# Nearest-neighbour upsampling on one core: the rows of x owned in two blocks instead of one

## The chip, the core and the metric

The kernel runs on one core of one Trainium2 chip. The metric is the device time of one execution in microseconds (us). The kernel before takes 197.16 us, the median of three runs that lie between 197.04 and 197.44 us. Lower is better.

## What is computed

The input x has the shape (16, 64, 64, 64) and the type float32. Each element of x becomes a square of two by two equal elements of the output, which has the shape (16, 64, 128, 128):

```python
for i in range(new_h):
    for j in range(new_w):
        result[:, :, i, j] = x[:, :, i // 2, j // 2].copy()
```

No arithmetic is done. 16.78 MB are read from DRAM and 67.11 MB are written to it.

## The kernel before

x is looked at as 65,536 rows of 64 floats (256 bytes each). One row of x makes 1,024 bytes of output: the widened row, twice. Partition p of the 128 partitions of SBUF owns 512 rows that follow each other, the rows 512p to 512p + 511. In x the first rows of two neighbouring partitions are therefore 128 KB apart, and in the output 512 KB.

One SBUF tile, `mem`, holds 207 KB a partition: a free region of 79 expanded rows at its start, and behind it the 512 rows of x (`xt`).

**Loads** (L149 to L151). SyncE (SP in the profile) issues three DMAs: rows 0 to 8 of each partition (256 KB in all, here called the head), rows 8 to 256 (7936 KB, the middle load) and rows 256 to 512 (8192 KB, the third load). `begin_before_barrier` (L13 to L33) takes the first `EARLY = 3` instructions of SP in the kernel's body and puts them ahead of the program's opening barrier.

**Expansion and stores** (L160 to L172). The rows are worked off in nine groups of 62, 32, 48, 64, 50, 64, 64, 64 and 64 rows a partition. For each group VectorE (DVE) copies the rows of x, broadcast in two axes, into an expanded buffer `u` inside `mem` (L170), and SP issues one DMA that stores `u` (L171). The buffers alternate between the start of `mem` and the place where rows of x have been used up (L162), so that the copy of a group waits for stores of earlier groups. The first group is copied in two parts, rows 0 to 31 and 31 to 62; its store waits for both. All twelve DMAs are issued by SP and go through one queue.

**The end** (L36 to L107). `close_early` rearranges the closing instructions: all semaphores but that of the last store are waited for and cleared early, and SP waits alone for the last store.

Of the kernel before, what the change touches and what calls it, by code (L numbers as in the profile page):

```python
# [1 line left out]

# [4 lines left out]

EARLY = 3  # L10


def begin_before_barrier(nc):  # L13

    blocks = nc.main_func.blocks
    main, body = blocks[0], blocks[1]
    sp = mybir.EngineType.SP
    loads = [i for i in body.instructions if i.engine == sp][:EARLY]  # L20
    for load in loads:
        assert isinstance(load, mybir.InstDMACopy), type(load)
        assert not (load.sync_info and load.sync_info.on_wait)
    names = [i.name for i in loads]
    body.instructions = [i for i in body.instructions if i.name not in names]
    kept = list(main.instructions)
    at = next(
        n
        for n, i in enumerate(kept)
        if i.engine == sp and isinstance(i, mybir.InstDrain)  # L30
    )
    kept[at:at] = loads
    main.instructions = kept  # L33


def close_early(nc):  # L36

    blocks = nc.main_func.blocks  # L40
    sp, pool = mybir.EngineType.SP, mybir.EngineType.Pool
    stores = [
        i
        for i in blocks[1].instructions
        if i.engine == sp and isinstance(i, mybir.InstDMACopy)
    ]
    last = stores[-1].sync_info.on_update[0].id

    end = list(blocks[-1].instructions)
    wait = end[0]  # L50
    assert wait.engine == sp and isinstance(wait, mybir.InstDrain)
    waits = list(wait.sync_info.on_wait)
    assert len({w.id for w in waits}) == len(waits) > 2
    assert all(w.wait_mode == "sem-ge-imm" for w in waits)

    mine = [i for i in end if i.engine == pool]
    kinds = [type(i).__name__ for i in mine]
    assert kinds == [
        "InstDrain",
        "InstEventSemaphore",  # L60
        "InstEventSemaphore",
        "InstDrain",
        "InstISA",
        "InstDrain",
        "InstEventSemaphore",
        "InstEventSemaphore",
    ], kinds
    d0, gather0, release0, d1, clear, d2, gather1, release1 = mine


    lo, hi = clear.ant_dict["range_first"], clear.ant_dict["range_last"]
    assert lo <= last <= hi and all(lo <= w.id <= hi for w in waits)
    clears = []
    for a, b in ((lo, last), (last + 1, hi + 1)):
        if a < b:
            clears.append(nc.gpsimd.sem_clear(range(a, b)).ins)

    landed = mybir.InstDrain(
        name=wait.name,
        engine=pool,  # L80
        debug=wait.debug,
        sync_info=mybir.SyncInfo(
            on_wait=[w for w in waits if w.id != last], on_update=[]
        ),
    )
    (w,) = [w for w in waits if w.id == last]
    final = mybir.InstEventSemaphore(
        name=clear.name,
        engine=sp,
        debug=wait.debug,  # L90
        sync_info=mybir.SyncInfo(
            on_wait=[w],
            on_update=[
                mybir.SyncUpdate(
                    sync_type=w.sync_type,
                    id=w.id,
                    ant_name=w.ant_name,
                    update_mode="sem-sub-imm",
                    update_value=w.wait_value,
                )  # L100
            ],
        ),
    )
    others = [i for i in end if i.engine != pool and i is not wait]
    blocks[-1].instructions = others + [
        d0, gather0, release0, gather1, release1, d1, landed, *clears, d2, final
    ]  # L107


@with_exitstack  # L110
def kernel(
    ctx: ExitStack,
    tc: tile.TileContext,
    x: bass.AP,
    scale_factor: int,
    out: bass.AP,
):
    nc = tc.nc
    nc.at_finalize(begin_before_barrier)
    nc.at_finalize(close_early)  # L120
    P = nc.NUM_PARTITIONS
    s = int(scale_factor)
    B, C, H, W = x.shape
    R = B * C * H // P
    fdt = x.dtype

    xp = x.rearrange("b c h w -> (b c h) w").rearrange("(p r) w -> p r w", p=P)
    op = out.rearrange("b c (h hd) w -> (b c h) (hd w)", hd=s).rearrange(  # L130
        "(p r) w -> p r w", p=P
    )

    rows = [62, 32, 48, 64, 50, 64, 64, 64, 64]
    GROW = s * s
    FREE = 79
    WF = FREE * GROW * W  # L140
    assert sum(rows) == R
    mem_pool = ctx.enter_context(tc.tile_pool(name="mem", bufs=1))
    mem = mem_pool.tile([P, WF + R * W], fdt, name="mem")
    xt = mem[:, WF:].rearrange("p (r w) -> p r w", r=R)

    HEAD = 8
    cuts = [0, HEAD, R // 2, R]  # L149
    for lo, hi in zip(cuts, cuts[1:]):  # L150
        nc.sync.dma_start(out=xt[:, lo:hi], in_=xp[:, lo:hi])  # L151

    def expanded(r0, r1):
        return (
            xt[:, r0:r1].unsqueeze(2).unsqueeze(4).to_broadcast([P, r1 - r0, s, W, s])
        )

    r0 = 0
    before = (0, 0)
    for n, k in enumerate(rows):  # L160
        size = k * GROW * W
        at = 0 if n % 2 == 0 else WF + r0 * W - size  # L162
        assert at >= before[1] or at + size <= before[0]
        before = (at, at + size)
        u = mem[:, at : at + size].rearrange(
            "p (k a w b) -> p k a w b", k=k, a=s, w=W
        )
        parts = [0, 31, k] if n == 0 else [0, k]
        for a, b in zip(parts, parts[1:]):
            nc.vector.tensor_copy(out=u[:, a:b], in_=expanded(r0 + a, r0 + b))  # L170
        nc.sync.dma_start(out=op[:, r0 : r0 + k, :], in_=u)  # L171
        r0 += k  # L172


# [1 line left out]
_INS = ['x', 'scale_factor']  # L176
_OUTS = [((16, 64, 128, 128), 'float32')]

_NUMBERS = {'scale_factor': 2}


# [26 lines left out]
```

## Time and profile before

| | |
|---|---|
| median of three runs | 197.16 us (197.04 to 197.44) |
| span of the profiled execution | 195.8 us |
| median time less that span | 1.36 us |
| VectorE busy | 78.0 us, 40% of the span |
| DMA queue: packets, bytes, share of 16 engines' span | 1728, 83.89 MB, 99.2% |
| packets under 512 B, under 2 KB, under 8 KB | 192, 192, 320 |

The span runs from the first to the last instruction of the one profiled execution. The page gives no time of its own for that execution, so the median stands beside its span, and the difference is what lies around the span. A DMA is cut into packets that 16 DMA engines carry; the packets under 512 B are the completion marks, 16 for each of the 12 DMAs, and the 128 between 2 KB and 8 KB are those of the head load (one for each partition, 2,048 B). In a table by stretches of time the columns are: the stretch and its length, busy time and count of each compute engine, the clock, the DMA share (the time of the packets that start in the stretch, over the stretch and 16 engines; it can pass 1) and GB/s (the bytes of the packets that start in it).

### The profile page before, as it was taken

How to read it: one execution, taken by the hardware profiler on the slowest of the kernel's cores; microseconds unless marked ns; L12 is line 12 of the kernel's file. 1: busy time of each engine (PE TensorE's matmuls, PEld its weight loads, DVE VectorE, ACT ScalarE, POOL GpSimd, SP SyncE). 2: the span in 40 equal slices, each digit the busy share in tenths (PEclk: the TensorE clock that was granted, in tenths of full speed). 3: DMA queues.
4: the chain of work that ended last, by engine and by line, in shares of the span. 5: the costliest groups of instructions: out<-in, count | busy, mean ns of one | idle time of the engine just before them, and what ended most of it. 6: DMA issues, size and time to landing. Idle time of an engine off the chain costs nothing.

```text
span 195.8 us, 76 instructions
## 1 busy us (share of the span) xinstructions
DVE 78.0 (40%) x10; POOL 0.2 (0%) x4
## 2 busy tenths in 40 slices
DVE  0000599980007579085008907900890088000000
POOL 0000000000000000000000000000000000000000
DMA  9999999999999999899987989999999999999994
GB/s 456 415 428 415 428 428 428 428 415 415 415 415 428 428 482 482 375 469 495 469 384 345 502 348 455 442 469 482 469 442 428 428 428 442 428 428 428 428 428 214
DMA packets 1728, 83.89 MB, mean 428 GB/s; under 512 B 192, under 2 KB 192, under 8 KB 320
## 3 DMA queue, kind: packets, MB, share of 16 engines
q1 hardware_dynamic: 1728, 83.89, 99.2%
HBM read 16.78 MB, written 67.11 MB: 428 GB/s over the span
## 4 chain that ended last, share of the span: by engine, by line
DMA 60%; DVE 24%; SPq 0%; issue 0%; DVEq 0%
DMA out_dram<-mem 49%; DVE mem L170 24%; DMA mem<-in_x_dram 11%; SPq L151 0%; DVEq L170 0%
## 5 line engine op out<-in xcount | busy, mean ns | idle before, releaser
L170 DVE COPY mem<-mem 128x16384 f32<-128x16384 f32 (+4 forms) x10 | 78.0, 7812 | 87.8 <-DMA out_dram<-mem 65.8
L189 POOL MEMSET const-uint8-127<- 128x1 uint8 x1 | 0.1, 102 | 0.0
L189 POOL MEMSET const-bfloat16-1.0<- 128x1 bf16 x1 | 0.1, 101 | 0.0
L189 POOL MEMSET const-float32-0.0<- 128x1 f32 x1 | 0.1, 98 | 0.2 <-issue 0.2
L189 POOL MEMSET const-float32-1.0<- 128x1 f32 x1 | 0.1, 98 | 0.0
## 6 DMA issues: line engine op xcount, KB each, us to landing
mem<-in_x_dram SPq DMA_DIRECT2D x1, 7936.0 KB, 21.5
out_dram<-mem SPq DMA_DIRECT2D x1, 7936.0 KB, 21.2
out_dram<-mem SPq DMA_DIRECT2D x1, 6400.0 KB, 27.6
out_dram<-mem SPq DMA_DIRECT2D x1, 6144.0 KB, 17.5
out_dram<-mem SPq DMA_DIRECT2D x1, 4096.0 KB, 26.4
mem<-in_x_dram SPq DMA_DIRECT2D x1, 256.0 KB, 2.7
out_dram<-mem SPq DMA_DIRECT2D x5, 29.8
mem<-in_x_dram SPq DMA_DIRECT2D x1, 40.4
```

Of the source, the lines that this page charges most:

```text
L170: nc.vector.tensor_copy(out=u[:, a:b], in_=expanded(r0 + a, r0 + b))
L189: nc = _bacc.Bacc("TRN2", target_bir_lowering=False, num_devices=1)
```

## The change

The ownership of rows is cut in two blocks. Partition p now owns 8 rows in the first 1,024 rows of x (rows 8p to 8p + 7) and 504 rows in the rest (1024 + 504p and on). The head load then reads one stretch of 256 KB of DRAM; in the second block the partitions lie 126 KB apart in x and 504 KB apart in the output. In SBUF nothing moves: the row numbers 0 to 511 of a partition, the groups and the copies are the same. The loads are still three DMAs of the same sizes. The first group has rows of both blocks, so its store becomes two DMAs: rows 8 to 62 first (6912 KB), then rows 0 to 8 (1024 KB, one stretch of the output). There are thirteen DMAs instead of twelve.

```diff
-    xp = x.rearrange("b c h w -> (b c h) w").rearrange("(p r) w -> p r w", p=P)
-    op = out.rearrange("b c (h hd) w -> (b c h) (hd w)", hd=s).rearrange(
-        "(p r) w -> p r w", p=P
-    )
+    xr = x.rearrange("b c h w -> (b c h) w")
+    outr = out.rearrange("b c (h hd) w -> (b c h) (hd w)", hd=s)
+    BLOCKS = [8, 504]
+    assert sum(BLOCKS) == R
+    xb, ob, r0 = [], [], 0
+    for k in BLOCKS:
+        xb.append(xr[P * r0 : P * (r0 + k)].rearrange("(p r) w -> p r w", p=P))
+        ob.append(outr[P * r0 : P * (r0 + k)].rearrange("(p r) w -> p r w", p=P))
+        r0 += k
+
+    def within(views, lo, hi):
+        found, r0 = [], 0
+        for k, v in zip(BLOCKS, views):
+            a, b = max(lo, r0), min(hi, r0 + k)
+            if a < b:
+                found.append((a, b, v[:, a - r0 : b - r0]))
+            r0 += k
+        return found
...
-    HEAD = 8
-    cuts = [0, HEAD, R // 2, R]
-    for lo, hi in zip(cuts, cuts[1:]):
-        nc.sync.dma_start(out=xt[:, lo:hi], in_=xp[:, lo:hi])
+    LOADS = [0, 8, R // 2, R]
+    for lo, hi in zip(LOADS, LOADS[1:]):
+        for a, b, part in within(xb, lo, hi):
+            nc.sync.dma_start(out=xt[:, a:b], in_=part)
...
-        nc.sync.dma_start(out=op[:, r0 : r0 + k, :], in_=u)
+        for a, b, part in reversed(within(ob, r0, r0 + k)):
+            nc.sync.dma_start(out=part, in_=u[:, a - r0 : b - r0])
```

## The prediction

> **What bounds the kernel now.** I read the DMA queue's line of the page first, then the chain of work that ended last, then the DMA issues with their sizes, and last the table by stretches of time around the start and the end.
>
> ```profile
> q1 hardware_dynamic: 1728, 83.89, 99.2%
> ```
>
> The packets fill 99.2% of the 16 engines' span: no compute engine matters unless it lets the queue run dry. The chain gives landings, as a start and a length:
>
> ```profile
> 0.00 0.38 SPq L151
> 0.38 0.05 issue
> 0.43 21.46 DMA mem<-in_x_dram
> ...
> 38.77 21.19 DMA out_dram<-mem
> 59.95 0.02 issue
> 59.98 6.57 DVE mem L170
> 66.55 0.02 issue
> 66.56 17.53 DMA out_dram<-mem
> ...
> 90.97 27.55 DMA out_dram<-mem
> ...
> 127.27 29.89 DMA out_dram<-mem
> ```
>
> ```profile
> mem<-in_x_dram SPq DMA_DIRECT2D x1, 7936.0 KB, 21.5
> out_dram<-mem SPq DMA_DIRECT2D x1, 7936.0 KB, 21.2
> out_dram<-mem SPq DMA_DIRECT2D x1, 6400.0 KB, 27.6
> out_dram<-mem SPq DMA_DIRECT2D x1, 6144.0 KB, 17.5
> out_dram<-mem SPq DMA_DIRECT2D x1, 4096.0 KB, 26.4
> mem<-in_x_dram SPq DMA_DIRECT2D x1, 256.0 KB, 2.7
> ```
>
> The middle load lands at 0.43 + 21.46 = 21.89 us, the first store at 59.96, the third (6144 KB) at 84.09, the fifth (6400 KB) at 118.52, the seventh at 157.16; the span ends at 195.8. Between those marks lie:
>
> - 21.89 to 59.96: the third load (8192 KB) and the first store, 16.52 MB in 38.07 us, 433.8 GB/s
> - 59.96 to 84.09: 10.49 MB in 24.13 us, 434.6 GB/s
> - 84.09 to 118.52: 14.94 MB in 34.43 us, 434.0 GB/s
> - 118.52 to 157.16 and 157.16 to 195.8: 16.78 MB in 38.64 us each, 434.2 GB/s
>
> One pace from 21.89 us to the end, through loads and stores and over every join of two DMAs. Nothing is to be had there. Up to 21.89 us the head and the middle load moved 8.39 MB, which at 434.2 GB/s take 19.32 us; **2.57 us are start-up**, paid once. The table by stretches shows what they are:
>
> ```profile
> 0.00:0.98 0.98, 0.00 (x0) 0.20 (x4) 1.00 0.00 0
> 0.98:1.22 0.24, 0.00 (x0) 0.00 (x0) 1.00 1.31 137
> 1.80:1.91 0.11, 0.00 (x0) 0.00 (x0) 1.00 1.00 391
> 2.41:2.60 0.19, 0.00 (x0) 0.00 (x0) 1.00 0.86 334
> 4.40:4.66 0.26, 0.00 (x0) 0.00 (x0) 1.00 4.54 1953
> 4.66:4.80 0.14, 0.00 (x0) 0.00 (x0) 1.00 7.32 3174
> 4.80:5.13 0.33, 0.00 (x0) 0.00 (x0) 1.00 0.00 0
> 5.13:5.15 0.02, 0.00 (x0) 0.00 (x0) 1.00 7.32 3174
> 57.10:57.24 0.14, 0.00 (x0) 0.00 (x0) 1.00 1.05 453
> 192.30:192.70 0.40, 0.00 (x0) 0.00 (x0) 1.00 5.67 2458
> 192.70:193.00 0.30, 0.00 (x0) 0.00 (x0) 1.00 0.00 0
> 193.00:193.05 0.05, 0.00 (x0) 0.00 (x0) 1.00 3.02 1311
> ```
>
> GB/s times the stretch is bytes, hence packets; share times 16 times the stretch is their time together. No packet starts in the first 0.98 us. In 0.98:1.22 start 32.9 KB, 16 head packets of 2,048 B, taking 1.31 x 16 x 0.24 = 5.03 us, **314 ns each**. In 1.80:1.91 start 21, in 1.76 us: **84 ns each**. So the head's first packets take almost four times what its last ones do. In 2.41:2.60 starts one packet of the middle load (63,488 B) and takes 2.61 us; the one in 57.10:57.24, of the same size but of a store, takes 2.35.
>
> Then count the middle load's second packets, one an engine: eight start in 4.40:4.66, seven in 4.66:4.80, none until 5.13, and the sixteenth in 5.13:5.15. **One engine is a third of a microsecond behind the other fifteen.** At the end it still is: fifteen of the last 65,536 B packets start in 192.30:192.70, none in 192.70:193.00, one in 193.00:193.05. Its packet takes 3.02 x 16 x 0.05 = 2.42 us, and about 0.35 us after that the span is over. All engines carry the same bytes at the same pace, so the engine that leaves the start-up last sets the end.
>
> **The change, part by part.** *The head load.* Same 256 KB, same 128 packets (SBUF takes 2,048 B a partition as before), same issue ahead of the others; only the DRAM addresses draw together. No row shows a load from one stretch. From below: the late engine and the slow first packets have nothing to do with the addresses, gain 0. From above: every engine leaves the start-up as early as the first ones do, 5.14 - 4.40 = 0.74 us. It can also lose, if 16 engines in one stretch get in each other's way; nothing excludes that, and the bound is the rival's below. I take the middle of the pack, because the fifteen other engines went through the same start-up in the same execution and are the nearest row: eight engines are through by 4.66, so the last one comes 5.14 - 4.66 = **0.48 us earlier**. My reason for a gain at all is the 314 against 84 ns: the excess sits where an engine touches DRAM first, at 16 places far apart, and with one stretch these first reads lie close together. This is argued and not shown.
>
> *The middle and third loads and eight of the stores* keep their sizes; their DRAM pitch goes from 128 to 126 KB and from 512 to 504 KB. The load at the one pitch and the stores at the other run at 433.8 and 434.2 GB/s: I count 0. The Trainium skill, page "DMA: Bandwidth & Descriptors", section "Latency and other measured facts", lists copies with a row pitch of 512 KiB at 207 GB/s and with a padded pitch at 214. By that rule the stores' 154.6 us at 434.2 GB/s would shrink by 3.3%, about 5 us by estimate; the trace disagrees so far, since 512 KB pitches already move at 434.2 GB/s beside 433.8 for a stretch that is half load at 128 KB.
>
> *The second store DMA.* Rows 0 to 8 leave as 128 packets of 8,192 B, eight an engine, behind those of rows 8 to 62. The bytes are the same, so what is added is the overhead of eight packets and one completion mark an engine. A 2,048 B packet takes 84 ns, while 2,048 B at a sixteenth of 434.2 GB/s (27.1) take 75.5: at most 8.5 ns a packet, 0.07 us for eight, and from below 0. A mark is a packet too; I give it one more such overhead. I take **0.06 us**, near the upper end.
>
> *The issue of that DMA.* SP is not counted as busy for it; the one issue in the chain took 0.38 us (0.00 on). It follows the first store's issue at 38.77, so SP is free by about 39.6. Behind it waits the second store's issue, which needs VectorE's third copy:
>
> ```profile
> 38.77 4.43 DVE L170 COPY mem<-mem 128x8192 f32<-128x8192 f32 x1
> 43.23 0.34 SPq L171 DMA_DIRECT2D out_dram<-mem  x1
> ```
>
> That is 43.2, so 3.6 us of cover; and the queue has the first 54 rows by then. Cost 0, and if the cover were gone, 0.38.
>
> *The added wait.* The third group's copy (59.98) overwrites the first store's buffer and must now wait for two DMAs. Both land by the time one did, plus the 0.06 above. Behind it stands the third store's issue at 66.56. Its 6144 KB need 14.5 us at the pace and land at 84.09, so it comes to move at about 69.6: 3 us after its issue, of which the 0.98 us before a first packet (the first stretch) must be taken off. Two microseconds hide the 0.06. With no such cover each 0.1 us of delay would be 0.1 us of dry queue.
>
> *The sum.* 195.8 - 0.48 + 0.06 = 195.4 us of span. Around the span lie 197.16 - 195.8 = 1.36 us if the profiled execution was one of the median, so **196.74 us**, 0.21% under it. What is late next is the slowest of the other engines.
>
> **The rivals.**
>
> *The start-up stays (no change).* The late engine's delay may come from how DMAs are handed to the engines and not from DRAM. For it: fifteen engines passed the same head within 0.4 us of each other, and the packet in 2.41:2.60 starts after all head traffic of the table's earlier rows, as if it had waited for its order. Against: the first packets are slow on many engines. Then only the added store counts: 197.16 + 0.06 = 197.22. A partial gain, the late engine catching up with half of its 0.34, gives 197.05. Within 0.2% (196.77 to 197.55, about what a measurement of this kernel can tell from no change) lies all of this.
>
> *Crowding (slower).* Sixteen engines read one 256 KB stretch instead of 16 places, and each packet then takes what only the first take now. Eight packets of 314 ns are 2.5 us an engine, where now the head lies between 0.98 and about 2.4, 1.4 us: 1.1 us more, 198.3. It decides as soon as the head costs 0.4 us more than now, a landing later than 2.7 + 0.4 = 3.1 us after its issue. For it: this addressing occurs nowhere in the trace. Against: 16 engines at equal offsets never disturb each other after 5 us.
>
> *Each DMA has its fixed price (slower).* The head's 256 KB land in 2.7 us, where 0.6 would do at the pace: 2.1 us. If the second store paid that, 197.16 + 2.1 = 199.3. The stretches speak against it: each has a join of two DMAs, none below 433.8 GB/s, where 2.1 us in 24.13 would be 9%. The Trainium skill, page "SBUF — State Buffer", section "The DMA setup-cost knee", has every transfer pay about 2 us and its summary says one DMA and not several; the head's row agrees, the queued stores' rows don't.
>
> *The pitch pays.* Stores 3% faster by some conflict that the trace doesn't show: 154.6 us less 3% is about 4.6 us, 192.5.
>
> *It doesn't do what it says.* The stretch might be carried in fewer, larger packets; the packet count shows it. The time would be that of the forecast or of no change.
>
> **How the numbers follow.** Forecast (start-up shorter by 0.4 to 0.8 us): 0.48. Start-up unchanged or little changed: 0.34. Crowding or any other longer start-up beyond 0.4 us: 0.15. Fixed price: 0.02. Pitch: 0.01. So faster 0.49, same 0.34, slower 0.17. The low end is the upper bound of the gain, 197.16 - 0.74 + 0.06 = 196.48, rounded down to 196.4 for the spread of the runs (0.12 below the median). The high end takes in no change and a start-up worse by some 0.4 us: 197.6. Outside are most of crowding, fixed price and pitch, some 0.17.
>
> **What would show it.** Right: packets 1872 (128 + 16 more), 208 of them under 512 B; the head landing earlier than 2.7 us; the middle load at about 21.4; the sixteen second packets close together and no gap like 4.80:5.13; later stretches still at 434 GB/s. Wrong: an engine still alone behind the others; a head landing past 3 us; a stretch with the two first stores below 433; an idle queue before 66.

## The result, and the profile after

The kernel after takes 197.55 us, the median of 22 runs (197.32 to 197.92), against 197.12 us for the kernel before in 22 runs beside them (196.97 to 197.78). The ratio is 1.002 with a 95% interval of 1.0014 to 1.0026: **0.4 us slower**, where 0.4 us faster was forecast. The profiled execution of the kernel after has a span of 196.2 us; the one before had 195.8.

The page of the kernel after, its DMA queue and its issues with the time to landing:

```profile
DMA packets 1872, 83.89 MB, mean 428 GB/s; under 512 B 208, under 2 KB 208, under 8 KB 336
...
q1 hardware_dynamic: 1872, 83.89, 99.2%
...
mem<-in_x_dram SPq DMA_DIRECT2D x1, 7936.0 KB, 21.7
out_dram<-mem SPq DMA_DIRECT2D x1, 6912.0 KB, 18.8
...
out_dram<-mem SPq DMA_DIRECT2D x1, 1024.0 KB, 20.9
mem<-in_x_dram SPq DMA_DIRECT2D x1, 256.0 KB, 2.7
```

The packets are as many as thirteen DMAs of unchanged form need, and the queue is as full as before. The head lands 2.7 us after its issue, as before. The middle load, with the same bytes, takes 21.7 us instead of 21.5.

The chain of work that ended last, kernel after (start, length, what):

```profile
0.42 21.71 DMA mem<-in_x_dram
...
39.40 20.87 DMA out_dram<-mem
...
66.94 17.49 DMA out_dram<-mem
...
91.31 27.57 DMA out_dram<-mem
...
127.63 29.85 DMA out_dram<-mem
```

Its landings stand against those of before like this: 22.13 against 21.89 (0.24 late), 60.27 against 59.96 (0.31), 84.43 against 84.09 (0.34), 118.88 against 118.52 (0.36), 157.48 against 157.16 (0.32), the end 0.4 late by the rounded spans. So **most of the loss is there by 22 us**; the stretch with the split store adds 0.07, and the rest of the kernel runs at the pace of before. The table by stretches of the kernel after shows the start and the last packets:

```profile
0.98:1.22 0.24, 0.00 (x0) 0.00 (x0) 1.00 1.27 179
1.22:1.50 0.28, 0.00 (x0) 0.00 (x0) 1.00 0.87 102
...
2.07:2.41 0.34, 0.00 (x0) 0.00 (x0) 1.00 8.34 3072
4.40:4.66 0.26, 0.00 (x0) 0.00 (x0) 1.00 1.69 733
4.66:4.80 0.14, 0.00 (x0) 0.00 (x0) 1.00 3.20 1360
4.80:5.13 0.33, 0.00 (x0) 0.00 (x0) 1.00 2.68 1154
5.13:5.50 0.37, 0.00 (x0) 0.00 (x0) 1.00 1.58 686
192.50:192.70 0.20, 0.00 (x0) 0.00 (x0) 1.00 3.03 1311
192.70:193.00 0.30, 0.00 (x0) 0.00 (x0) 1.00 2.52 1092
193.00:193.40 0.40, 0.00 (x0) 0.00 (x0) 1.00 2.65 1147
```

Read as in the prediction: of the middle load's sixteen second packets (63,488 B), three start in 4.40:4.66, three in 4.66:4.80, six in 4.80:5.13 and four in 5.13:5.50. Before it was fifteen by 4.80 and one later. **Ten engines are late instead of one**, the last of them at 5.42 us instead of 5.14, and they stay spread: of the last packets (65,536 B) four, five and seven start in the three last stretches. In 2.07:2.41 start all sixteen first packets of the middle load (1,016 of 1,044 KB) and fourteen of the head: 8.34 x 16 x 0.34 = 45.4 us, less 14 of 0.084, is 2.76 us for each. Before, in the stretch

```profile
1.91:2.60 0.69, 0.00 (x0) 0.00 (x0) 1.00 3.93 1558
```

of the kernel before, the same sixteen stand beside 29 head packets: (43.4 - 2.4) / 16 = 2.56 us. The middle load's first packets are 0.2 us longer on average. These are two single executions; what they can't tell apart, chance and layout, is left to the runs below.

### The profile page after: what moved, and what is told of

Its sections match the earlier page's. It is cut to its first block, busy times and chain, and to the rows that moved or that the text cites. A ratio compares the mean times of both kernels' runs of the same rounds, so it can differ in the third digit from the quotient of the medians.

```text
span 196.2 us, 79 instructions
## 1 busy us (share of the span) xinstructions
DVE 78.0 (40%) x10; POOL 0.2 (0%) x4
## 3 DMA queue, kind: packets, MB, share of 16 engines
q1 hardware_dynamic: 1872, 83.89, 99.2%
## 4 chain that ended last, share of the span: by engine, by line
DMA 60%; DVE 24%; SPq 0%; issue 0%; DVEq 0%
DMA out_dram<-mem 49%; DVE mem L179 24%; DMA mem<-in_x_dram 11%; SPq L160 0%; SPq L181 0%; DVEq L179 0%
## 6 DMA issues: line engine op xcount, KB each, us to landing
mem<-in_x_dram SPq DMA_DIRECT2D x1, 7936.0 KB, 21.7
```

## The experiments

The theories in the expectations: **A**, the middle load starts slowly because the head no longer reads the DRAM just ahead of it. **B**, sixteen engines crowd the head's one stretch. **C**, the pitch of the loads: 126 KB between the partitions is worse than 128. **D**, the second store DMA. **F**, the pitch of the stores. **G** was added later. Kernels of one group ran beside the same runs of the kernel before; each also has one profile, of one execution. Several kernels read or write at other addresses than the reference wants, so that one address pattern changes alone; the expectations say which rows are wrong.

| kernel | median us | before beside it | difference | ratio, 95% interval | engines after 4.80 us | last second packet at, us | span of that profile |
|---|---|---|---|---|---|---|---|
| e1 first store split | 197.39 | 197.24 | +0.15 | 1.0012 (0.9999 to 1.0026) | 3 | 5.33 | 196.6 |
| e2 head in one stretch | 197.14 | 197.24 | -0.10 | 1.0015 (0.9994 to 1.0036) | 4 | 4.94 | 195.8 |
| e3 head elsewhere | 197.08 | 197.24 | -0.16 | 0.9995 (0.9983 to 1.0007) | 6 | 5.35 | 196.5 |
| e5 blocks 504 and 8 | 197.46 | 197.24 | +0.22 | 1.0012 (1.0001 to 1.0023) | 8 | 5.39 | 196.3 |
| e4 both later loads at 126 KB | 197.42 | 197.20 | +0.22 | 1.0014 (0.9993 to 1.0034) | 5 | 5.20 | 196.0 |
| e7 stores by blocks | 197.15 | 197.20 | -0.05 | 0.9994 (0.9978 to 1.001) | 3 | 4.97 | 195.8 |
| e8 the kernel after again | 197.37 | 197.20 | +0.17 | 0.9997 (0.9972 to 1.0021) | 9 | 5.17 | 195.9 |
| e6 no head | 197.13 | 197.20 | -0.07 | 0.9987 (0.9971 to 1.0004) | other packets | 4.56 | 195.8 |
| e9 middle load 32 KB on | 197.14 | 197.14 | 0.00 | 0.9997 (0.9979 to 1.0014) | 1 | 4.81 | 195.7 |
| e10 middle load at 112 KB | 197.49 | 197.14 | +0.35 | 1.0009 (0.9986 to 1.0032) | 8 | 5.27 | 196.2 |
| e11 middle load at 126 KB | 197.47 | 197.14 | +0.33 | 1.001 (0.9998 to 1.0022) | 9 | 5.20 | 195.9 |
| e12 blocks 256 and 256 | 197.08 | 197.14 | -0.06 | 0.9999 (0.9989 to 1.0009) | 5 | 4.96 | 195.7 |
| f1 middle load at 96 KB | 197.46 | 197.15 | +0.31 | 1.0012 (0.9993 to 1.003) | 3 | 5.65 | 196.5 |
| f2 blocks 8, 256, 248 | 197.77 | 197.15 | +0.62 | 1.0025 (1.0012 to 1.0038) | other packets | 5.13 | 195.9 |
| f3 every store split | 197.77 | 197.15 | +0.62 | 1.0037 (1.002 to 1.0053) | 4 | 4.85 | 196.2 |
| g1 loads of f2 alone | 197.65 | 197.10 | +0.55 | 1.0028 (1.0016 to 1.0041) | other packets | 6.15 | 197.5 |
| g2 stores of f2 alone | 197.15 | 197.10 | +0.05 | 1.0002 (0.9992 to 1.0013) | 5 | 4.97 | 195.7 |
| g3 f2 again | 197.68 | 197.10 | +0.58 | 1.0025 (1.0008 to 1.0041) | other packets | 5.10 | 196.4 |

The difference is of the medians; the interval also takes in how widely the runs scatter, and single runs come one or two microseconds late, in the kernel before too; so the two don't always point the same way (e2). Most intervals of a single kernel hold 1, so what follows rests on groups of kernels. The last three columns are of the one profile: the number of the middle load's second packets that start between 4.80 and 5.90 us, the start of the last of them, and the span. In e6, f2, g1 and g3 those packets have 65,536 B ("other packets" in the count); in e6 no head stands ahead of them. The kernel before has 1, 5.14 us and 195.8 us, the kernel after 10, 5.42 and 196.2.

The span goes with the last of these packets and not with their number. Leave out f3 with its nine added DMAs and the three kernels with the loads of f2: where the last one starts by 4.97 us, the span is 195.7 to 195.8 us; at 5.14 to 5.20, 195.8 to 196.0; at 5.27 to 5.65, 196.2 to 196.6. With nine late engines e11 is done after 195.9 us, with three f1 takes 196.5. Two lines of each, f1 first, show the end of the start-up:

```profile
5.30:5.60 0.30, 0.00 (x0) 0.00 (x0) 1.00 0.00 0
5.60:5.70 0.10, 0.00 (x0) 0.00 (x0) 1.00 1.46 635
```

```profile
5.10:5.30 0.20, 0.00 (x0) 0.00 (x0) 1.00 0.73 317
5.30:5.60 0.30, 0.00 (x0) 0.00 (x0) 1.00 0.00 0
```

In f1 one engine (63,488 B) starts past 5.60; in e11 the last one starts before 5.30. And one profile is one draw: before, e1, e7, f3 and g2 have the same loads, and their last second packet starts anywhere from 4.85 to 5.33 us. So the profiles show where time is lost, and only the runs show which layout loses it.

**The first group: one part of the change at a time.**

e1, the split alone:

```diff
-        nc.sync.dma_start(out=op[:, r0 : r0 + k, :], in_=u)
+        halves = [(8, k), (0, 8)] if n == 0 else [(0, k)]
+        for a, b in halves:
+            nc.sync.dma_start(out=op[:, r0 + a : r0 + b, :], in_=u[:, a:b])
```

> Rows owned in one block as before; only the first store is cut into rows 8 to 62 and rows 0 to 8. Theory A (the middle load's first packets are slow because the head no longer reads the DRAM just ahead of them): the split costs only its packets, about 0.06 us, so 197.1 to 197.25 and the middle load lands at about 21.9 us as before. Rival D (the second store DMA is the cost): 197.5, the whole 0.4 us. Rivals B (16 engines crowd the one stretch of the head) and C (the pitch of 126 and 504 KB): as A.

+0.15 us: the interval reaches from zero to 0.5 us, so e1 alone excludes neither no cost nor D. The size of D was left to f3, which puts it at 0.07 us; as the only cause it falls there.

e2, the head's stretch alone:

```diff
+        src = xp[:, lo:hi]
+        if lo == 0:
+            src = x.rearrange("b c h w -> (b c h) w")[: P * HEAD].rearrange("(p r) w -> p r w", p=P)
-        nc.sync.dma_start(out=xt[:, lo:hi], in_=xp[:, lo:hi])
+        nc.sync.dma_start(out=xt[:, lo:hi], in_=src)
```

> Only the head load reads one stretch (the first 1024 rows of x); middle load, third load and stores keep the addresses of before, so rows 0 to 8 of a partition hold other data than the reference wants. Theory A: slower by 0.3 to 0.4 us (197.4 to 197.5), the middle load's first packets at 2.7 us on average or more, landing 0.2 to 0.3 later. Rival B: slower by as much, but with the head's own packets slower. Rival C (pitch) and D (store): no change, 197.1.

-0.10 us, though single late runs widen its interval to +0.7 us, so e2 alone doesn't exclude what A forecast; e3 does. B falls by the head itself, whose packets are not slower. The issues of e2's profile:

```profile
mem<-in_x_dram SPq DMA_DIRECT2D x1, 7936.0 KB, 21.2
...
mem<-in_x_dram SPq DMA_DIRECT2D x1, 256.0 KB, 2.4
```

The head did land earlier here, 2.4 us after its issue instead of 2.7, and that is nearly what I had hoped of the stretch. But the median time is that of before.

e3, a head that reads somewhere else at the old pitch:

```diff
+        at = R // 2 if lo == 0 else lo
-        nc.sync.dma_start(out=xt[:, lo:hi], in_=xp[:, lo:hi])
+        nc.sync.dma_start(out=xt[:, lo:hi], in_=xp[:, at : at + hi - lo])
```

> The head keeps its form and the 128 KB pitch but reads rows 256 to 264 of each partition's stretch, 62 KB behind the end of nothing that the middle load begins with; rows 0 to 8 hold other data than the reference wants. Theory A: slower by 0.3 to 0.4 us although nothing is in one stretch and no pitch is changed. Rivals B, C, D: no change, 197.1.

-0.16 us, with an interval that ends at +0.14 us. A falls: it doesn't matter whether the head has read near the middle load's first bytes.

e5, the two blocks in the other order (`BLOCKS = [504, 8]`), so that the pitch is there and the stretch is not:

> The two blocks in the other order: 504 rows a partition first, then 8 in the last 1024 rows of x. The head again reads just ahead of the middle load, now at 126 KB pitch; the third load and the last store are two DMAs each. Theory A: start-up as before, 0.06 to 0.12 us for the two added DMAs, 197.2; the middle load lands at about 21.9. Rival C (pitch): 197.5, as the kernel after. Rival B: 197.2. Rival D: 197.5 or more, two added DMAs.

+0.22 us with an interval above 1, and eight engines late. Two added DMAs are in this (about 0.07 each, see f3); not quite 0.1 us is left for the pitch, too little to tell from noise.

**The second group: loads against stores.** e4 reads the middle and the third load from the second block and leaves the rest:

```diff
+        src = xp[:, lo:hi]
+        if lo:
+            xr = x.rearrange("b c h w -> (b c h) w")
+            src = xr[P * HEAD :].rearrange("(p r) w -> p r w", p=P)[:, lo - HEAD : hi - HEAD]
-        nc.sync.dma_start(out=xt[:, lo:hi], in_=xp[:, lo:hi])
+        nc.sync.dma_start(out=xt[:, lo:hi], in_=src)
```

> The head as before (16 places 128 KB times four apart), the middle and third load from the second block (126 KB pitch), stores as before and not split; rows 8 to 512 hold other data than the reference wants. Theory C (the pitch of the loads makes the engines' first packets of the middle load end late): about 0.3 us slower than before, 197.5, with the second packets of the middle load spread past 4.80 us on many engines. Theory F (the pitch of the stores): no change. Theory D (the added store): no change.

e7 is the kernel after with the loads of before:

```diff
-        for a, b, part in within(xb, lo, hi):
-            nc.sync.dma_start(out=xt[:, a:b], in_=part)
+        nc.sync.dma_start(out=xt[:, lo:hi], in_=xr.rearrange("(p r) w -> p r w", p=P)[:, lo:hi])
```

> The loads as before in one block; only the stores go by blocks (504 KB pitch, first store in two DMAs), so rows land elsewhere than the reference wants. Theory C: only the split is paid, 0.05 to 0.15 us, as with the split alone. Theory F (the stores' pitch costs): 0.3 us or more, and the time is lost after 40 us and not before 5.

+0.22 for the loads' pitch, -0.05 for the stores' pitch with the split: F falls, since it forecast 0.3 or more and e7's interval ends at 0.2. C stands, though e4's interval holds 1. e4's profile has five late engines, no more than some kernels at the old pitch; the last one starts at 5.20 us.

> The kernel after, unchanged, beside the others on the same chip: 0.4 us slower than before by every theory. Its profile is a second look at the start-up: theory C expects the middle load's second packets again spread over about 1 us (4.4 to 5.4 us) on many engines; if only one engine is late this time, as in the kernel before, the spread was chance.

The kernel after again: +0.17 us by the medians here, 0.43 in the 22 runs of the result, so its size moves from one set of runs to the next; the interval of these 12 runs, up to 1.0021, does not even exclude zero. Its start-up in a second profile, second packets up to 4.80 us and after:

```profile
4.20:4.80 0.60, 0.00 (x0) 0.00 (x0) 1.00 1.73 741
4.80:5.90 1.10, 0.00 (x0) 0.00 (x0) 1.00 1.20 519
```

519 GB/s times 1.10 us are nine packets: the spread came back. But this execution is a fast one of its kernel, 197.22 us with a span of 195.9, and its middle load landed at 21.88 us, no later than before: nine late engines cost nothing, with the last of them at 5.17 us. Its head landed after 2.4 us, not 2.7 as in the first profile.

e6 drops the head (`EARLY = 2`, `cuts = [0, R // 2, R]`):

> No head load: two loads (rows 0 to 256 and 256 to 512), one block, stores as before. If the head's small packets take up a start-up delay that else the first large packets pay, the time stays within 0.1 us or rises; if the head itself costs (its packets' 84 ns against 75.5 and one more completion mark), 0.08 us are gained.

-0.07 us, no difference. Its second packets, sixteen of 65,536 B (1311 x 0.80), all start in one stretch:

```profile
3.90:4.70 0.80, 0.00 (x0) 0.00 (x0) 1.00 3.02 1311
```

**The third group: what about the pitch?** The middle load alone was moved. G: at 126 KB its packets cross 64 KB boundaries of x, at 128 they never did.

```diff
 # e9
+        at = lo + 128 if lo == HEAD else lo
-        nc.sync.dma_start(out=xt[:, lo:hi], in_=xp[:, lo:hi])
+        nc.sync.dma_start(out=xt[:, lo:hi], in_=xp[:, at : at + hi - lo])
 # e10; f1 has 384 in place of 448; e11 has the second block's view, as e4
+            src = xr[: P * 448].rearrange("(p r) w -> p r w", p=P)[:, lo:hi]
 # e12, in the kernel after
-    BLOCKS = [8, 504]
+    BLOCKS = [256, 256]
```

> As before, but the middle load reads rows 136 to 384 instead of 8 to 256 of each 128 KB stretch: the pitch stays, and each 62 KB packet now crosses a 64 KB boundary of x, as it does at 126 KB pitch and never did before; rows 8 to 256 hold other data than the reference wants. Theory G (what makes the first packets late at 126 KB pitch is that they cross such a boundary): 0.2 us slower than before, six or more engines start their second packet after 4.80 us. Theory C (what matters is that the 16 engines start at addresses that differ by powers of two): no change, at most four engines after 4.80 us.

> As before, but the middle load has a pitch of 112 KB, so the engines' first packets lie 448 KB apart, seven times 64 KB, and cross no 64 KB boundary; rows 8 to 256 hold other data than the reference wants. Theory C: 0.2 us slower, six or more engines after 4.80 us. Theory G: the first packets as before, at most four engines after 4.80 us.

> As before, but the middle load alone is read from the second block at 126 KB pitch; head, third load and stores as before; rows 8 to 256 hold other data than the reference wants. Theories C and G alike: as with the middle and the third load at that pitch, 0.2 us slower, six or more engines after 4.80 us. If the third load's pitch is what costs: no change, and at most four engines after 4.80 us.

> Two blocks of 256 rows a partition each: the middle load lies at 64 KB pitch, the third load is one stretch of 8 MB, the stores lie 256 KB apart, and no store is split, so twelve DMAs. Theories C and G: no change against before (197.1), at most four engines after 4.80 us. If every pitch but 128 KB costs, 0.2 us slower.

The second packets up to 4.80 us and after. e9:

```profile
4.20:4.80 0.60, 0.00 (x0) 0.00 (x0) 1.00 3.70 1587
4.80:5.90 1.10, 0.00 (x0) 0.00 (x0) 1.00 0.13 58
```

e10:

```profile
4.20:4.80 0.60, 0.00 (x0) 0.00 (x0) 1.00 1.95 847
4.80:5.90 1.10, 0.00 (x0) 0.00 (x0) 1.00 1.06 462
```

e11:

```profile
4.20:4.80 0.60, 0.00 (x0) 0.00 (x0) 1.00 1.71 741
4.80:5.90 1.10, 0.00 (x0) 0.00 (x0) 1.00 1.20 519
```

e12:

```profile
4.20:4.80 0.60, 0.00 (x0) 0.00 (x0) 1.00 2.70 1164
4.80:5.90 1.10, 0.00 (x0) 0.00 (x0) 1.00 0.67 289
```

One, eight, nine and five late engines; 0.00, +0.35, +0.33 and -0.06 us. G falls: e9 crosses the boundaries and loses nothing. (That e10 crosses none in its first packets rests on which partitions each engine begins with, and no run shows that.) By the times C holds in all four, and e11 shows that the middle load's pitch alone is enough; e12's five late engines are one more than C allowed.

Taken together the runs leave little doubt about the times. The 48 runs of e4, e10, e11 and f1 (below), in which the pitch of loads is 126, 112 or 96 KB and nothing else has changed, have a median 0.31 us above that of the kernel before beside them (95% interval by resampling the runs: 0.20 to 0.39). The 47 runs of e2, e3, e9 and e12, with pitches of 128 or 64 KB, lie 0.06 us below (-0.16 to +0.04).

**The fourth group.**

> As before, but the middle load at 96 KB pitch, so the engines' first packets lie 384 KB apart (three times 128 KB); rows 8 to 256 hold other data than the reference wants. Theory C in its strict form (the distance must be a power of two): 0.3 us slower, eight or more engines start their second packet after 4.80 us, as at 112 and 126 KB. Looser form (a common multiple of 128 KB between the engines is enough): no change, at most five.

+0.31 us with an interval that holds 1, and only three late engines. The time goes with the strict form of C, the count with the looser one. But the count is not what sets the time: one engine of f1 starts its second packet at 5.65 us, later than in any other kernel with packets of this size, and the span is 196.5 us. That speaks for the strict form; one profile and an interval that holds 1 don't settle it.

f3, nine added store DMAs (as e1, for every n):

> One block as before, and each of the nine stores in two DMAs (rows 8 on, then rows 0 to 8): nine added DMAs instead of one. If an added store DMA costs its eight packets and one mark, 0.05 us each: 0.45 us over before, 197.6. If one costs 0.15 us (the median of the run with one split): 1.35 us, 198.5. If nothing: 197.15.

+0.62 us for nine, **0.07 us each**. The chain of f3:

```profile
0.43 21.25 DMA mem<-in_x_dram
...
38.95 20.89 DMA out_dram<-mem
...
66.89 17.20 DMA out_dram<-mem
...
91.34 27.25 DMA out_dram<-mem
...
127.81 29.50 DMA out_dram<-mem
```

Between its landings at 21.68, 59.84, 84.09, 118.59 and 157.31 lie 38.16, 24.25, 34.50 and 38.72 us, against 38.07, 24.13, 34.43 and 38.64 before: 0.09, 0.12, 0.07 and 0.08 us for one, two, two and two added DMAs; the last stretch, to the end of the span, has two more and takes 38.9 us against 38.6.

f2 was to be the change mended: `BLOCKS = [8, 256, 248]` and `LOADS = [0, 8, 264, R]`.

> The change mended by theory C: three blocks of 8, 256 and 248 rows. The head is one stretch as in the kernel after, the first store is split as there, but the middle load has 256 rows at 64 KB pitch, so its engines start 256 KB apart; the third load (248 rows) has 62 KB pitch, and a second store is split (rows 256 to 264). Theory C: the 0.3 us of the pitch are gone, two splits are left, 0.1 us over before, 197.25. Rival (stretch and split are the cost): 0.4 us or more over before, 197.55.

It was not: +0.62 us. g1 has its loads with the stores of before (`outr.rearrange("(p r) w -> p r w", p=P)[:, r0 : r0 + k]` as the target, no split), g2 its stores with the loads of before, g3 is f2 again.

> The loads of the three blocks (8, 256 and 248 rows), the stores of the kernel before (one block, no split), so rows land elsewhere than the reference wants. If the loss of the three blocks is in the loads (against theory C, since the middle load lies at 64 KB pitch): 0.4 us or more over before. If it is in the stores: no change, 197.15.

> The loads of the kernel before, the stores of the three blocks (504 replaced by 256 and 248 KB between partitions, two stores split), so rows land elsewhere than the reference wants. If the loss of the three blocks is in the stores' addresses: 0.4 us or more over before, and the stores' pace after 100 us falls below that of before. If it is in the loads: two splits, 0.1 us, 197.25.

> The three blocks again, beside the two halves and for a second profile: 0.4 to 0.6 us over before if the first run was right; theory C expects 0.1 us, so if the first run's value stands, C does not explain all of what the blocks cost. A pace of the last stores below that of before would show where it goes.

The loss comes with the loads (g1 +0.55, g2 +0.05), but not all of it is there when they land. The chain of g3:

```profile
39.61 20.38 DMA out_dram<-mem
...
66.67 17.62 DMA out_dram<-mem
...
91.16 27.69 DMA out_dram<-mem
...
127.60 30.06 DMA out_dram<-mem
```

and of g2, which has the same stores:

```profile
38.96 20.84 DMA out_dram<-mem
...
66.48 17.49 DMA out_dram<-mem
...
90.85 27.55 DMA out_dram<-mem
...
127.15 29.93 DMA out_dram<-mem
```

g3 lands at 59.99, 84.29, 118.85 and 157.66 us, g2 at 59.80, 83.97, 118.40 and 157.08: 24.30 against 24.17, 34.56 against 34.43, 38.81 against 38.68. Each stretch of stores is 0.13 us longer in g3, though the loads are long done. The profile of f2, the same program in a faster execution (197.25 us), doesn't show this in its landings:

```profile
39.64 20.25 DMA out_dram<-mem
...
66.57 17.49 DMA out_dram<-mem
...
90.94 27.57 DMA out_dram<-mem
...
127.26 29.92 DMA out_dram<-mem
```

They lie 24.17, 34.45 and 38.67 us apart, as in g2. What all three profiles with these loads share is in the packet records of their traces: a store packet of 65,536 B takes 2,422 ns in the median and 2,424 on average in f2, g1 and g3, and 2,418 in the kernel before and in g2, where 99 of 100 take exactly that. Over all store packets of an engine that is 155.4 to 155.5 us against 155.0 (before) and 155.1 (g2). So some 0.3 to 0.5 us of added store time an engine follow from loads that are long done, about what f2, g1 and g3 lose beyond their splits in the medians; f2's fast execution, only 0.1 us over the span of before, shows that it need not all reach the end. f1 has it too (2,422 ns, 155.3 us), so its loss need not all be in the start-up; e4, e10 and e11 don't (2,418 ns, 155.0). Why is open. The blocks of f2 change the length of the middle load (256 rows) and the pitch of the third (62 KB) at once, and I did not part the two. So C accounts for the change as made, and not for every layout: f2's middle load lies at 64 KB, where its 256 rows make one unbroken stretch of x, and f2 loses all the same.

## Why the prediction was wrong, point by point

- **What bounds the kernel** was right: 99.2% of the queue before and after, one pace after the start, and the start-up as the part where most of the time moved.
- **The head load, 0.48 us earlier: this step failed, and its sign with it.** The stretch helps the head at times (2.4 us to landing in e2 and e8, 2.7 in the first profile of the change), but what an engine has ready at the end of the head does not set when the start-up ends. A head that lands 0.3 us earlier (e2), one that reads elsewhere (e3) and none at all (e6) gave -0.10, -0.16 and -0.07 us, all within noise. I took the long packets at 1 us for the cause of the late engine at 5 us; they were only ahead of it: in e8 the head's first sixteen packets take 101 ns each, not 314, and the last engine is at 5.17 us all the same. I also took one profile's late engine for a property of the kernel. With the same loads it starts at 5.14, 5.33, 4.97, 4.85 and 4.97 us (before, e1, e7, f3, g2), so the 0.48 us that I hoped to gain are the scatter from one execution to another.
- **The pitch at 0: this step failed too, and carries the loss.** I worked it out from the pace, 433.8 and 434.2 GB/s at two pitches. That pace is of engines already running. At the start sixteen first packets meet, and with 126, 112 or 96 KB between partitions the last engine came out of it at 5.17 to 5.65 us in seven profiles, with 128 or 64 KB at 4.81 to 5.14 in seven of nine, and at 5.33 and 5.35 in the two others, which are late executions of their kernels (e1, e3). In time: +0.22 (e4), +0.35 (e10), +0.33 (e11), +0.31 (f1), together 0.31 (0.20 to 0.39) for the loads' pitch alone, against -0.16 to 0.00 in e2, e3, e9 and e12. My evidence was two powers of two; neither bore on 126. That the power of two has to do with it is what the pitches tried suggest and no more, and it does not cover f2, whose middle load lies at 64 KB; what happens in the memory at the start isn't shown.
- **The rival that the pitch pays** fell: e7 and g2, with the stores at 504 KB and at 256 and 248 KB, stand at -0.05 and +0.05 us. The Trainium skill, page "DMA: Bandwidth & Descriptors", section "Latency and other measured facts", has copies slower at row pitches that are large powers of two; for these stores the runs show no difference, and for the loads 128 and 64 KB were better than 126, 112 and 96 KB, f2's loads apart.
- **The second store, 0.06 us: right.** 0.07 us in f3 by the times, 0.04 to 0.12 by the stretches. The rival of a fixed price of some 2 us for each DMA is out: nine would have cost 19 us and cost 0.62.
- **The issue and the added wait at 0: right.** The stretch 22.13 to 60.27 is 0.07 us longer than before and the next, 60.27 to 84.43, 0.03.
- **No change (0.34) and crowding (0.15)** were the rivals that came nearest. Crowding gave the sign by another mechanism, a head that would land late; it landed as before.
- **The sum** as measured: in the two profiles 0.24 us late when the middle load lands, 0.07 with the split store, the rest of the kernel about level. In the runs: 0.31 for the loads' pitch and 0.07 for the added store, 0.38 us, where 0.43 was measured.

## What to carry to other kernels

When a queue is full from end to end, only the start, the end and the overhead of each packet are left, and an edit there must be followed to the engine that comes out last and not to the first packets that look slow: an earlier head bought nothing here, and nine engines a little late cost nothing while the last of them was not later. Which engine is last, and by how much, changes from one execution to the next, so a single profile doesn't price a start-up; runs do. A change of addresses has to be priced at the start as well as at the steady pace, since the pace can hide a difference between the engines that stays with them to the end. An added DMA behind others in a full queue costs its packets, here 0.07 us, so a split is no reason against a layout, and no layout should be taken for neutral because the one that it replaces was.

## What the runs showed of the hardware that was not expected

- A spread among the sixteen engines at 5 us is carried through: in the kernel before one engine is about 0.3 us behind at 5 and at 193 us, in the kernel after the spread is still there in the last packets. The latest engine sets the span: 195.7 to 195.8 us where it starts its second packet by 4.97 us, 196.2 to 196.6 where it starts it at 5.27 to 5.65 (without f3 and the loads of f2).
- Loads with another layout can leave the stores that come after slower for the whole kernel: 2,422 ns for the median 65,536 B store packet in f1, f2, g1 and g3, against 2,418 in the kernel before and in g2.
- The Trainium skill, page "SBUF — State Buffer", section "The DMA setup-cost knee", states about 2 us for each transfer; the head alone, 2.7 us for 256 KB, agrees, while a DMA queued behind others cost 0.07 us in f3.
